# Lower-left blocks of the chunks' inverses two at a time in one product, and the sample rows' queries unpadded, in a GLA and RWKV-7 layer

## The chip, the cores and the metric

The kernel runs on one core of a Trainium2 chip. The metric is the device time of one execution in microseconds. The time before is the median of three runs, 1636.37 us (1636.02 to 1641.12).

## What is computed

One layer of a hybrid decoder for 1024 prompt rows and 8 sample rows of width 1024, all in float32. One input projection feeds two branches, gated linear attention (GLA, 4 heads with keys of 128 and values of 256) and RWKV-7 (16 heads of 64); their outputs go through an up projection each, are merged by gates, projected once more and normalised. The two parts that the change touches, from the reference:

```python
def step(S, inp):                        # RWKV-7, token by token
    rt, wt, kt, vt, kkt, at = inp
    sa = jnp.einsum('bhvk,bhk->bhv', S, -kkt)
    S = S * wt[:, :, None, :] + sa[..., None] * (kkt * at)[:, :, None, :] + vt[..., None] * kt[:, :, None, :]
    y = jnp.einsum('bhvk,bhk->bhv', S, rt)
    return S, y
...
# GLA: S_t = diag(a_t) S_{t-1} + k_t^T v_t ; o_t = q_t S_t
```

For a sample row there is one GLA step: its state (128 x 256 for each row and head) is decayed, gets one outer product added, and is read with the row's query.

## The kernel before, in words

The prompt is worked in two halves of 512 rows; the first half carries the 8 sample rows too (tiles of 260 columns, 512 in the second half). A float32 projection is made of three products in a rounded format, high times high, high times low and low times high (`xh`, `xl`, `whi`, `wlo`): for each piece of 512 weight columns a load `wraw`, a cast to `whi` on ACT and a difference `wlo` on DVE or POOL. In the first half both are also stored, and the second half loads them back.

RWKV-7 runs for 8 pairs of heads in each half, 16 pairs in all. The two heads of a pair lie in partitions 0 to 63 and 64 to 127. For a pair, `front` makes the chunked form: 8 chunks of 64 tokens, in which the recurrence becomes a triangular system. Its matrix's inverse is needed, transposed, in tile `XT` (chunk, head, 64 columns). `front` inverts the diagonal blocks of 32 x 32: it sends them from tile `GG` through memory (`LD`) to a layout with one block per partition, does 31 substitution steps on DVE with the scratch tile `Xt`, and brings the results back through `XD` into `XT`. What is left, the lower-left 32 x 32 block of each 64 x 64 inverse, is made in `back` by two products: the lower-left block of the matrix with one diagonal inverse (`pA`, copied to `As`), then the other diagonal inverse with that (`pZ`, copied to `XT`). Before the change each takes 8 matmuls, one per chunk, with a full 128 x 128 stationary operand and 64 columns streamed: of each head's 64 columns half are of use. `X1` holds the diagonal inverses transposed back, by two transposes of 32 x 256.

After `back`, `turn` transposes what the chain needs and `chain` goes through the 8 chunks one after the other, with three dependent products in tile `pch` each and copies between them.

For the samples, `gla_sample` is part of each of the 4 GLA heads in the first half. It spreads the 8 queries along a diagonal of a zeroed 64-column tile (`qm`), so that each sample's product streams 8 columns of which one isn't zero and all samples add up in one bank `po`. States and values are loaded for two samples at a time.

The order of the work is found by a planner in the program (class `Order`): every part is a stream that yields operations, and at each step the operation with the best key (its estimated start less a priority) is taken and put at the end of its engine's queue. Where an operation can run on two engines, the planner picks one. Buffers and banks come from pools (`big` has three banks). Because estimated starts decide, an edit at one place can move rows on every engine behind it. All DMAs are issued from SP, in order. Every operation is recorded from one line, L215, so the profile is read by tiles: `big<-X,gg` is the first product of `back`, `big<-XT,As` the second, `big<-row` with 8 columns the samples' product, `proj<-xh,whi` and its like the projections, `part,headsr` sums over a head.

Of the kernel before, what the change touches and what calls it, by code (L numbers as in the profile page):

```python
# [402 lines left out]
class Kern(Order):  # L403
# [71 lines left out]
    def setup(self):  # L475
# [65 lines left out]

        for tag, n, bufs in (("az", 4 * HT, 2), ("XT", 2 * HT, 2), ("X1", HT, 1), ("As", 2 * HT, 1)):
# [216 lines left out]
    def gla_head(self, c, h, rows, g):  # L759
# [105 lines left out]
        if c.i:  # L865
            yield S_.dma_start(self.o["gla_p"][0, 0, h], S)
        else:
            yield from self.gla_sample(h, q, k, v, al, [(AT_, z), (km_, vk1)], qp_)
# [24 lines left out]
    def gla_sample(self, h, q, k, v, al, bufs, qm_):  # L893
# [11 lines left out]

        qm = qm_[:, :NS * NS]
        yield E.memset(qm, 0.0)
        yield E.tensor_copy(qm[:, ::NS + 1], q[:, HT:])
# [10 lines left out]
        po = yield from self.bank("big", [P, 2, NS])  # L919
        for n in range(NS // W):  # L920
            Sg, vb = (x[:, :W * GDV].rearrange("p (b v) -> p b v", b=W) for x in bufs[n % 2])
            for w in range(W):
                b = n * W + w
                t = HT + b
                yield A.activation(vb[:, w], vb[:, w], AF.Copy, scale=k[:, t:t + 1])
                yield V.scalar_tensor_tensor(Sg[:, w], Sg[:, w], al[:, t:t + 1], vb[:, w], ALU.mult, ALU.add)
                for j in range(2):
                    yield self.P.matmul(po[:, j], Sg[:, w, j * P:(j + 1) * P], qm[:, NS * b:NS * b + NS],
                                        start=(b == j == 0), stop=(b == NS - 1 and j == 1))
            yield self.S.dma_start(self.o["gla_s"][0, n * W:n * W + W, h].rearrange("b k v -> k b v"), Sg)  # L930
            if n + 2 < NS // W:
                yield from load(n + 2)
        for j in range(2):
            yield self.C.copy(v[j][:, HT:], po[:, j])
        self.free(po)
# [98 lines left out]
    def front(self, c, p, st, d):  # L1034
# [103 lines left out]
        d.AZ, d.BK, d.G, d.XT, d.v, d.bonus, d.pc, d.L = AZ, BK, GG, XT, st[2], st[1], pc, L_  # L1138
        d.y = Pc_[:, :HT]

    def back(self, d):
        GG, XT = d.G, d.XT

        X1_, As_ = (yield from self.get("X1")), (yield from self.get("As"))
        X1 = X1_.rearrange("p (c h t) -> p c h t", c=NCH, h=2)
        As = As_.rearrange("p (c h t) -> p c h t", c=NCH, h=2)
# [12 lines left out]

        for h, hs in enumerate(HS):  # L1160
            yield self.C.copy(XT[q[2 * h], :, h, 32:64], pZ[q[2 * h], :, h])
# [501 lines left out]
```

## Time and profile before

| What | Value |
|---|---|
| median of 3 runs | 1636.37 us |
| profiled execution | 1634.97 us |
| its span, first to last instruction | 1633.0 us |
| mean granted TensorE clock | 0.989 |
| DMA, mean | 193 GB/s |
| DMA issues on SP's queue | 1461 |

One execution was taken by the hardware profiler. "Busy" is the time in which an engine had an instruction running, as a share of the span; a row of a group gives the engine, the operation, the tile written and the tiles read, shapes, the count, then the busy time in microseconds, the mean length of one in ns, and the idle time of the engine just before them with what ended it. The granted clock is the share of TensorE's full clock.

### The profile page before, as it was taken

How to read it: one execution, taken by the hardware profiler on the slowest of the kernel's cores; microseconds unless marked ns; L12 is line 12 of the kernel's file. 1: busy time of each engine (PE TensorE's matmuls, PEld its weight loads, DVE VectorE, ACT ScalarE, POOL GpSimd, SP SyncE). 2: the span in 40 equal slices, each digit the busy share in tenths (PEclk: the TensorE clock that was granted, in tenths of full speed). 3: DMA queues.
4: the chain of work that ended last, by engine and by line, in shares of the span. 5: the costliest groups of instructions: out<-in, count | busy, mean ns of one | idle time of the engine just before them, and what ended most of it. 6: DMA issues, size and time to landing. Idle time of an engine off the chain costs nothing.

```text
span 1633.0 us, 29970 instructions
## 1 busy us (share of the span) xinstructions
PE 1580.9 (97%) x10130; PEld 1404.8 (86%) x10130; DVE 1309.8 (80%) x3396; ACT 880.3 (54%) x2112; POOL 116.0 (7%) x204
## 2 busy tenths in 40 slices
PE   8999999799999998999999999999999999999998
PEld 7899999799999898788888877778878889988786
DVE  7788898889887897679788898989887886656565
ACT  5546766576485757464636472447254758554210
POOL 2100010001000101000000011201000100000000
PEclk9999999899999999999999999999999999999999
DMA  9878775676678556653465446445653577788432
GB/s 292 257 222 251 240 217 157 201 250 191 196 242 264 166 173 210 204 190 120 140 192 161 133 156 200 120 141 178 193 167 117 175 224 253 230 282 270 151 110 84
DMA packets 311924, 315.26 MB, mean 193 GB/s; under 512 B 75363, under 2 KB 197356, under 8 KB 311772
## 3 DMA queue, kind: packets, MB, share of 16 engines
q1 hardware_dynamic: 311772, 313.36, 61.7%
q8 instruction: 80, 1.31, 0.3%
q14 instruction: 72, 0.59, 0.1%
HBM read 195.45 MB, written 117.82 MB: 192 GB/s over the span
## 4 chain that ended last, share of the span: by engine, by line
PE 73%; DVE 14%; DMA 6%; ACT 4%; issue 2%; SPq 1%; POOL 0%; DVEq 0%; POOLq 0%; ACTq 0%
PE proj L215 41%; PE big L215 20%; PE pY L215 7%; PE pch L215 4%; DVE row L215 4%; DVE wide L215 2%; DMA wide<-LD 2%; ACT row L215 1%; DVE X L215 1%; SPq L215 1%; DVE az L215 1%; DMA wraw<-w_in 1%; DVE wlo L215 1%; DVE Xt L215 1%; ACT wide L215 1%
## 5 line engine op out<-in xcount | busy, mean ns | idle before, releaser
L215 PE MATMUL proj<-xh,whi 128*128 128x260 f32 (+1 forms) x1880 | 618.2, 329 | 1.1 <-DVE row L215 0.7
L215 PE MATMUL proj<-xl,whi 128*128 128x260 f32 (+1 forms) x1880 | 617.6, 328 | 0.2 <-DVE xl L215 0.2
L215 PE MATMUL proj<-xh,wlo 128*128 128x260 f32 (+1 forms) x1880 | 616.6, 328 | 0.7 <-POOL wlo L215 0.5
L215 PEld LDWEIGHTS proj<-xh,whi 128*128 128x128 f32 x1880 | 356.6, 190 | 28.5 <-issue 2.6
L215 PEld LDWEIGHTS proj<-xh,wlo 128*128 128x128 f32 x1880 | 356.2, 189 | 26.3 <-issue 2.1
L215 PEld LDWEIGHTS proj<-xl,whi 128*128 128x128 f32 x1880 | 356.4, 190 | 24.8 <-issue 2.6
L215 DVE TENSOR_TENSOR wlo<-wraw,whi 128x512 fp32r<-128x512 f32 x204 | 141.4, 698 | 42.7 <-ACT whi L215 40.3
L215 ACT CAST whi<-wraw 128x512 fp32r<-128x512 f32 x210 | 129.1, 620 | 81.4 <-PE proj L215 34.7
L215 DVE TENSOR_TENSOR row<-row 128x512 f32<-128x512 f32 (+9 forms) x317 | 158.7, 504 | 7.7 <-ACT row L215 3.0
L215 ACT ACTIVATE row<-row 128x512 f32<-128x512 f32 (+5 forms) x229 | 138.3, 611 | 32.5 <-DVE row L215 17.6
L215 DVE TENSOR_TENSOR Xt<-X,wide 128x60 f32<-128x60 f32 (+24 forms) x496 | 104.9, 212 | 31.2 <-DMA wide<-LD 20.5
L215 DVE TENSOR_TENSOR X<-X,Xt 128x60 f32<-128x60 f32 (+24 forms) x496 | 108.2, 218 | 11.4
L215 PE MATMUL big<-row 128*128 128x64 f32 (+4 forms) x712 | 115.0, 278 | 2.1 <-DVE X L215 1.2
L215 ACT ACTIVATE s0p<-wide,pc 64x64 f32<-64x64 f32 x256 | 88.0, 344 | 49.4 <-DVE wide L215 45.4
L215 PEld LDWEIGHTS big<-row 128*128 128x128 f32 (+1 forms) x712 | 97.1, 191 | 7.4 <-DVE row L215 2.7
L215 ACT COPY wide<-pch 64x64 f32<-64x64 f32 x221 | 45.6, 206 | 107.0 <-PE pch L215 103.0
L215 ACT ACTIVATE row<-proj,omu 128x260 f32<-128x260 f32 (+1 forms) x99 | 54.1, 546 | 89.8 <-PE proj L215 84.0
L215 POOL TENSOR_TENSOR row<-row 128x512 f32<-128x512 f32 (+7 forms) x52 | 60.0, 1156 | 560.8 <-DVE row L215 204.5
L215 DVE SCALAR_TENSOR_TENSOR row<-proj,pv,row 128x259 f32<-128x259 f32 (+1 forms) x99 | 56.4, 570 | 34.4 <-ACT tail L215 18.5
L215 ACT COPY wide<-wide 32x256 f32<-32x256 f32 x181 | 73.0, 403 | 18.1 <-DVE wide L215 16.0
L215 DVE SCALAR_TENSOR_TENSOR wide<-pch,pc,s0p 64x64 f32<-64x64 f32 x224 | 63.0, 281 | 21.1 <-PE pch L215 16.8
L215 ACT COPY row<-big 128x128 f32<-128x128 f32 (+7 forms) x162 | 45.4, 309 | 49.1 <-PE big L215 47.4
(259 smaller groups left out, 2770.0 us busy)
## 6 DMA issues: line engine op xcount, KB each, us to landing
wraw<-w_in SPq DMA_DIRECT2D x146, 256.0 KB
wh<-whi SPq DMA_DIRECT2D x146, 256.0 KB
wl<-wlo SPq DMA_DIRECT2D x146, 256.0 KB
whi<-wh SPq DMA_DIRECT2D x146, 256.0 KB
wlo<-wl SPq DMA_DIRECT2D x146, 256.0 KB
wide<-LD SPq DMA_DIRECT2D x64, 128.0 KB
wraw<-w_up_gla SPq DMA_DIRECT2D x32, 256.0 KB
wraw<-w_up_rwkv SPq DMA_DIRECT2D x32, 256.0 KB
```

The lines of the kernel that those rows point to most:

```text
L215: ways.append((eng, lambda call=call: call(out, *args, **kw), price(eng, name, out, args, ins)))
```

## The change

In `front`, six more DMAs per pair. Four bring the lower-left blocks of `GG` into a new tile `L1` (4 x 128 columns, zeroed once): chunk x of the first four and chunk x + 4 of the last four, for both heads, stand in its four 32 x 32 blocks beside the diagonal. Two bring the second diagonal inverse of the last four chunks into the free upper right part of `XT`.

In `back`, both products run over x = 0 to 3 instead of 0 to 7: 4 matmuls of 32 columns with `L1`, and 4 of 64 columns with `As`, which is now 4 x 128 columns. The transposes are 4 of 32 x 128 and go to the scratch tile `Xt`; the tile `X1` is gone. The copies out of each product are 4 of 32 x 128 instead of 2 of 32 x 256.

In `gla_sample`, `qm` with its memset and copy is gone. Each sample's product streams its one query column; a bank of 2 x 2 columns is taken for each group of two samples, copied by two copies of 128 x 2 into the rows' place, and freed, four times a head.

```diff
         for q in range(4):
             yield self.S.dma_start(XD.rearrange("u (i g) t -> g u i t", g=4)[q], X[NU * q:NU * q + NU])
         self.free(X_)
+        L1 = (yield from self.get("L1")).rearrange("p (x t) -> p x t", t=P)
+        H = NCH // 2
+        for h in range(2):
+            for n in range(2):
+                g, to = 2 * h + n, 2 * h + 1 - n
+                yield self.S.dma_start(L1[32 * g:32 * g + 32, :, 32 * to:32 * to + 32],
+                                       GG[64 * h:64 * h + 32, H * n:H * n + H, 0, h, 32:64])
...
+        for h in range(2):
+            yield self.S.dma_start(XT[64 * h:64 * h + 32, 0:H, h, 32:64],
+                                   XD[(2 + h) * NCH + H:(3 + h) * NCH].rearrange("c s t -> s c t"))
...
         for h in range(2):
-            yield self.V.transpose(X1[q[2 * h], :, h], XT[q[2 * h], :, h, 0:32])
-        pA = yield from self.bank("big", [P, NCH, 2, 32])
-        for x in range(NCH):
-            yield self.P.matmul(pA[:, x], GG[:, x, 0], X1[:, x], start=True, stop=True)
+            for n in range(2):
+                yield self.V.transpose(X1[q[2 * h + n]], XT[q[2 * h], H * n:H * n + H, h, 0:32])
+        pA = yield from self.bank("big", [P, H, 32])
+        for x in range(H):
+            yield self.P.matmul(pA[:, x], d.L1[:, x], X1[:, x], start=True, stop=True)
         for h in range(2):
-            yield self.C.copy(As[q[2 * h + 1], :, h, 0:32], pA[q[2 * h + 1], :, h])
-        self.free(pA, X1_)
-        pZ = yield from self.bank("big", [P, NCH, 2, 32])
-        for x in range(NCH):
+            for n in range(2):
+                g = 2 * h + 1 - n
+                yield self.C.copy(As[q[g], :, q[2 * h + n]], pA[q[g]])
+        self.free(pA, X1_, d.L1)
+        pZ = yield from self.bank("big", [P, H, 2, 32])
+        for x in range(H):
             yield self.P.matmul(pZ[:, x], As[:, x], XT[:, x, :, 32:64], start=True, stop=True)
+        for h in range(2):
+            for n in range(2):
+                yield self.C.copy(XT[q[2 * h], H * n:H * n + H, h, 32:64], pZ[q[2 * h + n], :, h])
...
-        qm = qm_[:, :NS * NS]
-        yield E.memset(qm, 0.0)
-        yield E.tensor_copy(qm[:, ::NS + 1], q[:, HT:])
...
         for n in range(NS // W):
+            po = yield from self.bank("big", [P, 2, W])
...
                 for j in range(2):
-                    yield self.P.matmul(po[:, j], Sg[:, w, j * P:(j + 1) * P], qm[:, NS * b:NS * b + NS],
-                                        start=(b == j == 0), stop=(b == NS - 1 and j == 1))
+                    yield self.P.matmul(po[:, j, w:w + 1], Sg[:, w, j * P:(j + 1) * P], q[:, t:t + 1],
+                                        start=(w == j == 0), stop=(w == W - 1 and j == 1))
+            t = HT + n * W
+            for j in range(2):
+                yield self.C.copy(v[j][:, t:t + W], po[:, j])
+            self.free(po)
```

How the planner's order stands now is shown at three places. In its rows `X_184` is the tile `X1`, `L_184` is `L1`, a number ahead of a row is its place on the engine, and xN counts equal instructions in a row.

DVE, third pair of the first half, before: `az_177` and `wide` are the next pair's `front`, `wlo` a piece of weights.

```order
558 L215 SCALAR_TENSOR_TENSOR row<-row,nkk 128x512
559 L215 TENSOR_SCALAR row<-row,pv,oka 128x512
560 L215 TENSOR_TENSOR az_177<-row 64x8x64 x2
561 L215 COPY gg<-az_176 64x8x64 x2
562 L215 SCALAR_TENSOR_TENSOR row<-row 128x512
563 L215 TENSOR_TENSOR row<-row 128x512
564 L215 TENSOR_TENSOR az_177<-row 64x8x64 x2
565 L215 COPY pc<-row 128x8
566 L215 TENSOR_TENSOR wide<-row 64x8x64 x4
567 L215 SCALAR_TENSOR_TENSOR row<-row,pv 128x512
568 L215 TENSOR_TENSOR wlo<-wraw,whi 128x512
```

DVE at the same place now, from a piece of weights ahead of the copy to `As`:

```order
546 L215 TENSOR_TENSOR wlo<-wraw,whi 128x512
547 L215 SCALAR_TENSOR_TENSOR row<-row,pv 128x512 x2
548 L215 CAST l2p<-l2s 128x256
549 L215 COPY As_186<-big 32x4x32
550 L215 SCALAR_TENSOR_TENSOR row<-proj,pv,row 128x251
551 L215 SCALAR_TENSOR_TENSOR row<-bnd,pv,row 128x1
552 L215 SCALAR_TENSOR_TENSOR smp<-shT,pv,row 128x8
553 L215 TENSOR_TENSOR row<-row 128x512
554 L215 TENSOR_TENSOR wlo<-wraw,whi 128x512
555 L215 COPY gg<-az_176 64x8x64 x2
```

Ten rows stood between the copy to `As` (557, not shown) and the next piece of weights; now four stand between, and the next pair's `az` rows come later.

TensorE, second pair of the first half, before: the first product of `back` stands at row 1358, the second here.

```order
1369 L215 MATMUL proj<-xh_199,whi 128x260
1370 L215 MATMUL proj<-xl_217,whi 128x260
1371 L215 MATMUL big<-alr_144,gw_146 128x260
1372 L215 MATMUL big<-XT_181,As_186 128x64 x8
1373 L215 MATMUL big<-alr_144,gw_146 128x260
```

TensorE, the same pair now:

```order
1310 L215 MATMUL proj<-xl_315,whi 128x260
1311 L215 MATMUL proj<-xh_286,wlo 128x260
1312 L215 MATMUL big<-Xt,L_184 128x32 x4
1313 L215 MATMUL big<-XT_181,As_186 128x64 x4
1314 L215 MATMUL proj<-xh_199,whi 128x260
```

Thirteen rows stood between the two products, and none stands there now. The fourth pair has the same neighbours now (rows 2335 and 2336), and the sixth pair had them before.

TensorE at the end of the first half, before, when its projections are used up and the chain's products are left:

```order
3934 L215 MATMUL proj<-xh_286,wlo 128x260
3935 L215 MATMUL pch<-rh,XT_180 128x128
3936 L215 MATMUL pch<-wide 128x128
3937 L215 MATMUL pY<-gg,wide 128x128
3938 L215 MATMUL pch<-wide,gg 128x128
3939 L215 MATMUL pY<-az_176,wide 128x128
3940 L215 MATMUL pch<-rh,XT_180 128x128
3941 L215 MATMUL pch<-wide 128x128
3942 L215 MATMUL pY<-gg,wide 128x128
3943 L215 MATMUL pch<-wide,gg 128x128
```

TensorE there now, where the last projection stands at row 3939 and the products at 3940 to 3944 are those of 3935 to 3939 above:

```order
3945 L215 MATMUL pch<-rh,XT_180 128x128
3946 L215 MATMUL pch<-wide 128x128
3947 L215 MATMUL pY<-gg,wide 128x128
3948 L215 MATMUL pch<-wide,gg 128x128
3949 L215 MATMUL pY<-az_176,wide 128x128
3950 L215 MATMUL pch<-rh,XT_180 128x128
3951 L215 MATMUL big<-part,headsr 128x512
3952 L215 MATMUL pch<-wide 128x128
```

After the last projection five products of `pch` followed the first one (3936, 3938, 3940, 3941, 3943); now it is seven (3941, 3943, 3945, 3946, 3948, 3950, 3952).

More of the change, by code (lines that the diff above doesn't have):

```diff
@@ L540, in setup @@
             nc.gpsimd.memset(t, 0.0)
-        for tag, n, bufs in (("az", 4 * HT, 2), ("XT", 2 * HT, 2), ("X1", HT, 1), ("As", 2 * HT, 1)):
+        for tag, n, bufs in (("az", 4 * HT, 2), ("XT", 2 * HT, 2), ("L1", HT, 1), ("As", HT, 1)):
             ts = [cp.tile([P, n], F32, name=f"{tag}{i}") for i in range(bufs)]
@@ L867, in gla_head @@
         else:
-            yield from self.gla_sample(h, q, k, v, al, [(AT_, z), (km_, vk1)], qp_)
+            yield from self.gla_sample(h, q, k, v, al, [(AT_, z), (km_, vk1)])
         s0, s1 = z, vk1
@@ L891, in gla_head, with gla_sample @@
         self.headed += 1
-    def gla_sample(self, h, q, k, v, al, bufs, qm_):
+    def gla_sample(self, h, q, k, v, al, bufs):
         a, A, V, E = self.a, self.A, self.V, self.E
@@ L918, in gla_sample @@
         yield from load(1)
-        po = yield from self.bank("big", [P, 2, NS])
         for n in range(NS // W):
+            po = yield from self.bank("big", [P, 2, W])
             Sg, vb = (x[:, :W * GDV].rearrange("p (b v) -> p b v", b=W) for x in bufs[n % 2])
@@ L932, in gla_sample @@
                 yield from load(n + 2)
-        for j in range(2):
-            yield self.C.copy(v[j][:, HT:], po[:, j])
-        self.free(po)
     def lora(self, c):
```

10 lines of the change are left out of this document (5 added, 5 removed).

## The prediction

> **What bounds the kernel now.** I read the page first, then the groups by form, then TensorE's timeline around one pair's two products, then the long breaks.
>
> ```profile
> PE 1580.9 (97%) x10130; PEld 1404.8 (86%) x10130; DVE 1309.8 (80%) x3396; ACT 880.3 (54%) x2112; POOL 116.0 (7%) x204
> PEclk9999999899999999999999999999999999999999
> PE 73%; DVE 14%; DMA 6%; ACT 4%; issue 2%; SPq 1%; POOL 0%; DVEq 0%; POOLq 0%; ACTq 0%
> ```
>
> TensorE is busy in 97% of the span and carries 73% of the chain that ended last. Idle are 1633.0 - 1580.9 = 52 us. The large products hardly wait for anything:
>
> ```profile
> L215 PE MATMUL proj<-xh,whi 128*128 128x260 f32 (+1 forms) x1880 | 618.2, 329 | 1.1 <-DVE row L215 0.7
> L215 PE MATMUL proj<-xl,whi 128*128 128x260 f32 (+1 forms) x1880 | 617.6, 328 | 0.2 <-DVE xl L215 0.2
> L215 PE MATMUL proj<-xh,wlo 128*128 128x260 f32 (+1 forms) x1880 | 616.6, 328 | 0.7 <-POOL wlo L215 0.5
> ```
>
> 5640 of them show 2.0 us of idle time in all: operands are there when TensorE comes to them. So the sum is first a count of TensorE's work, then of its few breaks.
>
> **The products of the inverse.** Here are pair 0's two, in TensorE's timeline (start, length, count of records; an f32 matmul leaves two records):
>
> ```profile
> 130.87 0.28 PE L215 MATMUL proj<-xl,whi 128*128 128x260 f32 x1
> 130.99 1.89 PE L215 MATMUL big<-X,gg 128*128 128x64 f32 x16
> 132.69 0.37 PE L215 MATMUL proj<-xh,wlo 128*128 128x260 f32 x1
> ...
> 134.09 0.28 PE L215 MATMUL proj<-xl,whi 128*128 128x260 f32 x1
> 134.21 1.89 PE L215 MATMUL big<-XT,As 128*128 128x64 f32 x16
> 135.91 0.37 PE L215 MATMUL proj<-xh,wlo 128*128 128x260 f32 x1
> ```
>
> From its own start to the next start, each step takes 132.69 - 130.99 = 1.70 us for 8 matmuls, and 1.70 again: 0.106 us a record. The change leaves 4 matmuls of each. The first also shrinks from 64 to 32 columns; what a 32-column record takes, no row shows. It lies between the 64-column row and the 8-column one:
>
> ```profile
> 314.07 0.51 PE L215 MATMUL big<-row 128*128 128x8 f32 x4
> 314.44 0.37 PE L215 MATMUL proj<-xl,whi 128*128 128x260 f32 x1
> ```
>
> That is (314.44 - 314.07)/4 = 0.093 us at 8 columns. Between 8 and 64 columns the pace hardly moves, so I take 0.106: 0.85 us instead of 1.70. With 16 pairs and two steps, 32 x 0.85 = **27.2 us off TensorE**; at 0.093 for the first step it would be 16 x 8 x 0.013 = 1.7 us more.
>
> **The samples' products.** 64 matmuls go from 8 columns to 1. By the two rows above, 56 columns fewer are worth 13 ns, so 7 fewer are worth under 2 ns: 128 records x 2 ns = 0.3 us. I take nothing. What is removed for each of four heads, a memset and a copy on POOL or DVE, frees an engine that is 7% or 80% busy and releases no projection. Added are 24 small copies out of PSUM on ACT or DVE, and the bank is asked for four times in each head instead of being held throughout. ACT has 46% of its time free; nothing taken. If that cover is gone, a copy that is late delays the next group's store and load on SP's queue, and no projection.
>
> **Copies and transposes.** Per pair, 2 transposes become 4 of half the size, and 2 + 2 copies become 4 + 4.
>
> ```profile
> L215 DVE STREAM_TRANSPOSE X<-XT 32x256 f32<-32x256 f32 x32 | 13.8, 432 | 2.1 <-DMA XT<-XD 1.4
> L215 ACT COPY As<-big 32x256 f32<-32x256 f32 x30 | 10.9, 365 | 20.6 <-PE big L215 20.3
> L215 ACT COPY XT<-big 32x256 f32<-32x256 f32 x30 | 10.9, 362 | 25.6 <-PE big L215 25.3
> ```
>
> The transposes now write Xt, the scratch tile of the substitution, so this step of one pair and the substitution of the next could wait for each other.
>
> ```profile
> L215 DVE TENSOR_TENSOR Xt<-X,wide x1: 193/193/193, 164.4 to 164.4; 128x31 f32<-128x31 f32 x1
> ```
>
> Pair 1's substitution starts at 164.4, 28 us after pair 0's second step is over, and in the changed order the 31 steps of a pair and its 4 transposes strictly alternate: nothing. Half-size pieces cost between half and the whole of these: 0 to 0.86 us more of DVE and 0 to 1.45 us more of ACT per pair (4 more copies at no more than 0.363), 23 us of ACT over the kernel at most, inside 750 us in which it is free. On TensorE they count only where the second step stands right behind the first; that is priced below.
>
> **The new DMAs.** 4 + 2 more on SP's queue per pair, 96 in all.
>
> ```profile
> L215 SPq DMA_DIRECT2D XT<-XD x64: 323/450/837, 123.9 to 1351.3; - x64
> ```
>
> ```profile
> SPq L215 <- PE proj L215: 285.0, 128, 8.5
> ```
>
> The first row gives an issue's time (least, median, most), 0.45 us: 2.7 us a pair, 43 us in all. The second says that SP stood 285.0 us behind TensorE's projections, 128 times. All six stand ahead of weight loads and stores. They are covered by the 285 us in which SP itself waits for TensorE to give weight buffers back. I take nothing here; it is the slower rival below.
>
> **The breaks.** The change leaves no row of the schedule where it was, so I price each long break of before and ask the order whether it is still there. Windows: length, busy time of PE, PEld, DVE, ACT, POOL, granted clock.
>
> ```profile
> 288.20:296.90 8.70, 0.25 (x3) 0.04 (x1) 8.59 (x15) 3.31 (x9) 1.28 (x1) 0.63 0.25 92
> 296.90:305.00 8.10, 8.08 (x29) 7.20 (x30) 6.17 (x9) 4.07 (x10) 2.35 (x6) 0.56 0.63 195
> 538.00:550.00 12.00, 10.44 (x62) 10.10 (x61) 11.86 (x20) 7.23 (x18) 1.80 (x2) 0.72 0.41 138
> ...
> 543.00:549.80 6.80, 6.80 (x33) 6.80 (x33) 6.73 (x13) 2.62 (x7) 0.53 (x1) 0.50 0.11 40
> ...
> 640.00:656.00 16.00, 11.23 (x43) 7.46 (x42) 14.41 (x29) 8.75 (x24) 3.90 (x7) 0.68 0.40 129
> ```
>
> At 288 TensorE stands 8.45 us while DVE is full: the stretch of DVE rows 558 to 567, with no piece of weights among them. Then it runs 8.1 us at a clock of 0.56, which loses 8.1 x 0.44 = 3.6 us: 12.0 us. In the changed order the next front starts later and DVE's rows at this place have pieces of weights at 546 and 554; I take the break as gone, **-12.0 us** (ends: 0 and -12.0).
>
> At 538 the second step stands right behind the first:
>
> ```profile
> 538.71 0.28 PE L215 MATMUL proj<-xh,wlo 128*128 128x260 f32 x1
> 539.36 2.00 PE L215 MATMUL big<-X,gg 128*128 128x64 f32 x16 [0.38 <-DVE X L215]
> 542.54 3.30 PE L215 MATMUL big<-XT,As 128*128 128x64 f32 x16 [1.18 <-ACT As L215]
> ```
>
> Idle 12.00 - 10.44 = 1.56 us, clock 12 x 0.28 = 3.4 us: 4.9 us. Before has one such place, after has two (second and fourth pair; rows 1312 and 1313 show the second): **+4.9 us** (ends: 0 and +9.8). Here the clock was 0.50 from 543.0 on, after breaks of 0.38 and 1.18 us. The Trainium skill, "TensorE: Matmul & The Clock Gate", Part 1, speaks against the price: it has the clock halve only after an idle window of about 3.4 us; by that rule such a place would cost its idle 1.6 us, and this term would be +1.6. The measurement decides.
>
> At 640 the first half's projections are used up and the chain runs alone: idle 16.00 - 11.23 = 4.77 us, clock 16 x 0.32 = 5.1 us, over five products of the chain with no projection between them (rows 3936 to 3943): 2.0 us each. After has seven (3941 to 3952): **+4.0 us** (ends: 0 and +6).
>
> Last, a new order brings breaks that I can't point to. I allow one of the size of 538's, **+4.9 us** (ends: 0 and one like 288's, +12.0).
>
> **Sum.** -27.2 - 12.0 + 4.9 + 4.0 + 4.9 = -25.4 us. The profiled execution took 1634.97 us (span 1633.0 and 2.0 around it), so 1609.6; the median of the runs stands 1.4 above it: **1611 us**.
>
> **Rivals.**
> *SP's queue becomes the bound (slower).* 96 issues x 0.45 = 43.2 us. If every one delayed a weight piece for which TensorE then waits, 43.2 - 27.2 = +16: 1652 us. It decides once the lead is used up: in the first half a weight piece serves 24 products 0.12 us apart (130.87 to 130.99 above is one), 2.9 us, so four buffers serve 11.5 us. Six issues are 2.7 us, so the queue must already be 9 us behind. For it: the six come in a burst, some wait for landings. Against: the 2.0 us of idle at the projections, and the 285 us. Chance 0.07.
> *Waits take the gain's place.* DVE is at 80% overall, and at 8.59 of 8.70 us in the break at 288; a faster TensorE meets it more often. Two breaks like 288's that I don't see, 24 us, would leave 1611 + 24 = 1635, no change: 0.07. One, with the 288 break itself still there in another place, 1623: 0.15, still faster.
> *The columns set the pace.* If a record cost what it streams, 0.12/260 = 0.46 ns a column, the first step would save 16 x 0.030 - 8 x 0.015 = 0.36 us a pair and the second 0.24: 9.6 us, with the other terms 1629. The Trainium skill, "TensorE: Matmul & The Clock Gate", section Back-to-back issue gap, lists a floor of about 25 ns for 1 to 64 columns; by it 256 records fewer would be worth an estimated 6.4 us. The rows show 0.106 us at 64 columns and 0.093 at 8, so no pace by column: 0.02.
>
> **How the numbers follow.** The forecast has 0.69. A measurement of this kernel tells about 0.3%, 4.9 us, from no change. Faster by more: 0.69 + 0.15 + 0.02 = 0.86; within: 0.07; slower: 0.07. The lower end takes the break at 288 as gone and nothing new: 1636.4 - 27.2 - 12.0 = 1597, less 2 for a cheaper 32-column record: 1595. The upper end keeps 288's break, the two short places at 9.8 and the boundary at +6, and one small new break of 4.9: 1636.4 - 27.2 + 20.7 = 1630, or 1629 with the cheaper record. About 0.15 is left above, little below.
>
> **What would show it.** Right: 128 records in each of the two groups, the steps 0.85 us from start to next start, some 256 records fewer on TensorE, projections still with about 2 us of idle, no window of 8 us idle in the first 400 us, the first two back-to-back places at a half clock. Wrong: a 32-column step near 0.4 us (columns), SP with far less waiting for TensorE and projections with tens of microseconds of idle behind weight pieces (the queue), or TensorE's idle time grown by 20 us with DVE as releaser (waits).

## The result and the profile after

The changed kernel takes 1652.96 us (median of 5 runs, 1648.70 to 1658.57) against 1637.01 us for the kernel before (5 runs, 1636.02 to 1641.12). The ratio is 1.0104, interval 1.0087 to 1.0120: slower by 16 us, where 25 us faster was forecast.

The page of the changed kernel, its engines' busy times, the granted clock and the chain's shares:

```profile
PE 1570.7 (95%) x9874; PEld 1390.4 (84%) x9874; DVE 1311.1 (79%) x3385; ACT 895.1 (54%) x2210; POOL 143.8 (9%) x223
PEclk9999999999998999899999999999999999999999
PE 66%; DVE 14%; DMA 8%; ACT 5%; SPq 3%; issue 3%; POOL 0%; POOLq 0%; DVEq 0%; ACTq 0%
```

The 256 records are gone as forecast, but TensorE's busy time fell by only 10.2 us. Its idle time rose from 52.1 to 1649.3 - 1570.7 = 78.6 us, and the mean clock fell from 0.989 to 0.980. A lower clock hides in the busy time: 1649.3 x 0.020 = 33.0 us of it, against 1633.0 x 0.011 = 18.0 us before. Busy time less that is TensorE's work at full clock: 1562.9 us before and 1537.7 after. So **25.2 us of work did go**, and 26.5 us of idle time and 15.0 us of clock came, which is the 16.3 us by which the span grew.

TensorE's timeline at pair 0's two products (start, length, count of records):

```profile
134.48 0.98 PE L215 MATMUL big<-Xt,L 128*128 128x32 f32 x8
135.29 0.37 PE L215 MATMUL proj<-xh,whi 128*128 128x260 f32 x1
...
137.18 1.00 PE L215 MATMUL big<-XT,As 128*128 128x64 f32 x8
137.99 0.37 PE L215 MATMUL proj<-xh,whi 128*128 128x260 f32 x1
```

135.29 - 134.48 = 0.81 us and 137.99 - 137.18 = 0.81 us: each step has half its former length, at 32 columns as at 64.

The same view at the second pair, where the two products now stand one behind the other (in brackets: idle before, and what ended it):

```profile
206.56 1.08 PE L215 MATMUL big<-Xt,L 128*128 128x32 f32 x8 [3.12 <-DVE Xt L215]
208.79 1.97 PE L215 MATMUL big<-XT,As 128*128 128x64 f32 x8 [1.15 <-ACT As L215]
```

Windows of the changed kernel (length; busy time of PE, PEld, DVE, ACT, POOL; clock; DMA): the second pair, the place of the old break at 288, the fourth pair, and the end of the first half:

```profile
200.00:214.00 14.00, 9.73 (x61) 9.42 (x60) 12.75 (x21) 7.61 (x20) 3.37 (x3) 0.77 0.63 185
280.00:305.00 25.00, 24.25 (x195) 23.59 (x195) 16.25 (x35) 21.77 (x52) 0.80 (x2) 1.00 0.94 300
372.00:386.00 14.00, 8.57 (x50) 8.23 (x49) 13.81 (x22) 5.35 (x16) 4.46 (x8) 0.76 0.83 253
640.00:672.00 32.00, 26.43 (x144) 20.87 (x144) 24.43 (x54) 18.33 (x48) 3.43 (x7) 0.84 0.42 150
```

The last of these in the kernel before:

```profile
640.00:672.00 32.00, 26.79 (x155) 21.51 (x154) 22.20 (x50) 14.07 (x41) 3.90 (x7) 0.84 0.50 150
```

The break at 288 is gone. The second and fourth pair cost 4.27 + 14 x 0.23 = 7.5 us and 5.43 + 14 x 0.24 = 8.8 us. The end of the first half costs what it did: 5.6 us idle against 5.2, at the same clock.

One more break stands at products of the samples. The same window in the changed kernel and in the kernel before:

```profile
515.00:533.00 18.00, 12.60 (x68) 11.37 (x67) 14.62 (x57) 8.04 (x22) 0.12 (x1) 0.72 0.65 215
```

```profile
515.00:533.00 18.00, 18.00 (x142) 17.37 (x141) 15.76 (x55) 8.69 (x20) 0.00 (x0) 1.00 0.85 266
```

That is 5.4 us of idle time and 18 x 0.28 = 5.0 us of clock, 10.4 us, where before has none. Two of the rows that wait there in the changed kernel, and two of ACT's beside them (`issue` means that the profile shows nothing that was waited for):

```profile
522.61 0.98 PE L215 MATMUL big<-row 128*128 128x1 f32 x4 [2.33 <-issue]
526.25 1.02 PE L215 MATMUL big<-row 128*128 128x1 f32 x4 [1.32 <-DVE row L215]
```

```profile
524.96 0.22 ACT L215 COPY row<-big 128x2 f32<-128x2 f32 x2 [2.58 <-PE big L215]
525.07 0.92 ACT L215 ACTIVATE row<-row 128x256 f32<-128x256 f32 x2
```

ACT's copies out of one group's bank, which the change added, wait for that group's products, and the two rows behind them are part of the next group's states, for which the product at 526.25 waits.

The projections, which waited 2.0 us in all:

```profile
L215 PE MATMUL proj<-xh,whi 128*128 128x260 f32 (+1 forms) x1880 | 620.8, 330 | 9.9 <-DMA whi<-wh 8.0
L215 PE MATMUL proj<-xh,wlo 128*128 128x260 f32 (+1 forms) x1880 | 619.9, 330 | 0.6 <-POOL wlo L215 0.5
L215 PE MATMUL proj<-xl,whi 128*128 128x260 f32 (+1 forms) x1880 | 617.9, 329 | 0.2 <-DVE xl L215 0.2
```

Now they wait 10.7 us, 8.0 of it for weights that the second half loads back. SP's timeline at one of those places, then SP's own wait for TensorE and the issue time of the loads into the tile L1:

```profile
795.05 2.54 SPq L215 DMA_DIRECT2D XD<-X  x4
797.64 2.54 SPq L215 DMA_DIRECT2D L<-gg  x4
800.34 2.91 SPq L215 DMA_DIRECT2D XT<-XD  x6
803.35 0.38 SPq L215 DMA_DIRECT2D whi<-wh  x1
```

```profile
SPq L215 <- PE proj L215: 254.6, 128, 8.3
```

```profile
L215 SPq DMA_DIRECT2D L<-gg x64: 586/600/1809, 119.9 to 1366.1; - x64
```

Fourteen issues stand in one piece, 8.3 us, and the load of `whi` behind them is late, although SP still has 254.6 us in which it waits for TensorE: that free time lies elsewhere.

What one such late load costs, in TensorE's timeline and in windows behind it:

```profile
806.23 0.50 PE L215 MATMUL proj<-xh,whi 128*128 128x512 f32 x1 [2.28 <-DMA whi<-wh]
```

```profile
806.20:808.20 2.00, 1.98 (x13) 1.80 (x14) 0.00 (x0) 0.39 (x2) 0.00 (x0) 1.00 0.73 121
808.20:812.00 3.80, 3.80 (x15) 3.20 (x14) 0.79 (x3) 2.68 (x6) 0.00 (x0) 0.55 1.03 364
812.00:815.00 3.00, 3.00 (x14) 2.42 (x13) 2.97 (x6) 2.71 (x6) 0.00 (x0) 1.00 0.64 203
```

2.28 us of idle time, and 2 us later a mean clock of 0.55 over 3.8 us, another 1.7 us. The kernel has four such waits, 8.0 us, and the clock falls behind each: its mean is 0.81, 0.79, 0.69 and 0.68 over the 9.0, 8.1, 11.0 and 10.6 us that begin with them (from 719.0, 803.9, 1044.0 and 1211.4 us), 10.2 us in all. The Trainium skill, "TensorE: Matmul & The Clock Gate", Part 1, lets the clock halve after an idle window of about 3.4 us; here it fell behind a break of 2.28 us, and the measurement decides. The length of a break alone does not settle it, though. A break of 2.24 us in the same trace left the clock at 1.00:

```profile
918.59 0.46 PE L215 MATMUL pch<-wide 128*128 128x128 f32 x2 [2.24 <-DVE wide L215]
```

```profile
914.00:926.00 12.00, 9.76 (x54) 8.09 (x53) 8.77 (x31) 4.72 (x13) 0.00 (x0) 1.00 0.59 157
```

### The profile page after: what moved, and what is told of

Read it like the earlier page. It is cut to its first block, busy times and chain, and to the rows that moved or that the text cites. A ratio compares the mean times of both kernels' runs of the same rounds, so it can differ in the third digit from the quotient of the medians.

```text
span 1649.3 us, 29754 instructions
## 1 busy us (share of the span) xinstructions
PE 1570.7 (95%) x9874; PEld 1390.4 (84%) x9874; DVE 1311.1 (79%) x3385; ACT 895.1 (54%) x2210; POOL 143.8 (9%) x223
## 4 chain that ended last, share of the span: by engine, by line
PE 66%; DVE 14%; DMA 8%; ACT 5%; SPq 3%; issue 3%; POOL 0%; POOLq 0%; DVEq 0%; ACTq 0%
PE proj L215 36%; PE big L215 19%; PE pY L215 7%; PE pch L215 4%; DVE row L215 4%; SPq L215 3%; DVE wide L215 2%; DVE Xt L215 2%; ACT row L215 2%; ACT wide L215 2%; DMA wide<-LD 2%; DVE X L215 2%; DVE az L215 1%; DMA whi<-wh 1%; DMA l2s<-lora 1%
## 5 line engine op out<-in xcount | busy, mean ns | idle before, releaser
L215 PEld LDWEIGHTS proj<-xl,whi 128*128 128x128 f32 x1880 | 358.3, 191 | 24.4 <-issue 1.7
L215 DVE TENSOR_TENSOR wlo<-wraw,whi 128x512 fp32r<-128x512 f32 x198 | 137.5, 700 | 47.5 <-ACT whi L215 44.5
L215 DVE TENSOR_TENSOR row<-row 128x256 f32<-128x256 f32 (+9 forms) x305 | 153.1, 505 | 8.9 <-ACT row L215 2.2
L215 ACT ACTIVATE row<-row 128x512 f32<-128x512 f32 (+4 forms) x229 | 138.0, 611 | 25.9 <-DVE row L215 15.8
L215 DVE TENSOR_TENSOR Xt<-X,wide 128x60 f32<-128x60 f32 (+24 forms) x496 | 108.5, 219 | 24.3 <-DMA wide<-LD 12.2
L215 POOL TENSOR_TENSOR row<-row 128x512 f32<-128x512 f32 (+6 forms) x64 | 71.0, 1112 | 547.3 <-DVE row L215 279.0
L215 ACT ACTIVATE s0p<-wide,pc 64x64 f32<-64x64 f32 x256 | 88.1, 344 | 42.9 <-DVE wide L215 39.0
L215 ACT COPY wide<-wide 32x256 f32<-32x256 f32 x193 | 77.8, 403 | 18.4 <-DVE wide L215 16.1
L215 DVE SCALAR_TENSOR_TENSOR row<-proj,pv,row 128x259 f32<-128x259 f32 (+1 forms) x99 | 56.4, 570 | 26.3 <-ACT tail L215 13.8
```

The source lines that it names most:

```text
L215: ways.append((eng, lambda call=call: call(out, *args, **kw), price(eng, name, out, args, ins)))
```

## The experiments

Two theories stood at the start: the new order brings the breaks, or the six DMAs per pair do. The run kept_half put a third in their place: TensorE's saved time is not worth its length in this kernel. All runs in numbers follow. The ratios are to the kernel before on the same chip, and the other columns are worked out from the page and the clock of the profiled execution as above (a clock is given to 0.001, so work is good to about 1 us).

| Run | Ratio [95%] | Idle us | Clock loss us | Work at full clock us |
|---|---|---|---|---|
| before | 1 | 52.1 | 18.0 | 1563 |
| after | 1.0104 [1.0087, 1.0120] | 78.6 | 33.0 | 1538 |
| kept_order | 1.0267 [1.0237, 1.0297] | 90.6 | 55.4 | 1532 |
| products_only | 1.0122 [1.0084, 1.0161] | 81.0 | 33.0 | 1536 |
| samples_only | 1.0058 [1.0037, 1.0079] | 56.9 | 18.1 | 1570 |
| no_six | 1.0015 [0.9999, 1.0031] | 69.6 | 27.8 | 1538 |
| planned_without | 1.0049 [1.0029, 1.0069] | 73.7 | 31.1 | 1533 |
| l1_early | 1.0138 [1.0108, 1.0167] | 85.5 | 34.7 | 1533 |
| before_nudge | 1.0074 [1.0046, 1.0102] | 55.7 | 29.6 | 1559 |
| after_nudge | 1.0034 [1.0018, 1.0050] | 72.7 | 31.2 | 1536 |
| kept_half | 0.9993 [0.9979, 1.0006] | 67.8 | 24.4 | 1537 |
| kept_no_six | 1.0023 [1.0009, 1.0038] | 74.4 | 31.2 | 1538 |
| pool_six | 1.0075 [1.0057, 1.0092] | 77.8 | 33.0 | 1537 |
| kept_pool | 1.0100 [1.0078, 1.0123] | 78.6 | 31.3 | 1540 |
| less_dve | 0.9978 [0.9965, 0.9990] | 50.8 | 19.6 | 1561 |
| less_both | 0.9961 [0.9948, 0.9975] | 65.7 | 26.0 | 1534 |
| more_pe | 1.0104 [1.0087, 1.0122] | 42.9 | 16.5 | 1590 |
| after_less | 1.0118 [1.0099, 1.0138] | 74.1 | 41.3 | 1537 |
| no_az | 0.9932 [0.9916, 0.9949] | 46.1 | 17.8 | 1559 |
| no_az_half | 0.9860 [0.9843, 0.9877] | 56.6 | 17.7 | 1535 |

The last column falls into three groups: 1559 to 1570 with whole products, 1532 to 1540 with halved ones, 1590 with half of them doubled. What differs inside a group is idle time and clock.

In several runs the planner is shown an operation of the kernel before, so that the order stays, while other instructions are issued in its place; `put` does that. The pieces of code below are shortened.

**Order or DMAs.** kept_order keeps every engine's order as before and issues the change in it; the new loads go behind old ones.

```diff
-                yield self.S.dma_start(o, x)
+                yield put(self.S.dma_start(o, x), lambda e: (sync.dma_start(o, x), sync.dma_start(lo, li)))
...
-            yield self.P.matmul(pA[:, x], GG[:, x, 0], X1[:, x], start=True, stop=True)
+            yield put(self.P.matmul(pA[:, x], GG[:, x, 0], X1[:, x], ...), lambda e: matmul(pAn[:, x], L1[:, x], Xn[:, x]) if x < H else None)
```

> The planner is shown the operations of before, so every engine keeps the order of before; only what is issued is the change's: 4 matmuls instead of 8 in both steps, the small transposes and copies in place of the large ones, the six DMAs right behind XD's and XT's, the samples' queries one column each (in one bank, copied out at the end as before). Theory 1, the new order makes the breaks: 27 us less work in an order that had few breaks, 1608 to 1618 us. Theory 2, the six DMAs make SP late wherever they stand: no gain, 1635 to 1655 us.

products_only is the changed kernel with the old `gla_sample`, samples_only the kernel before with the new one:

```diff
-            yield from self.gla_sample(h, q, k, v, al, [(AT_, z), (km_, vk1)], qp_)
+            yield from self.gla_sample(h, q, k, v, al, [(AT_, z), (km_, vk1)])
```

> The change's products and DMAs with the samples as before; the planner is free. Theory 1: yet another order, so anywhere between a full gain and the loss of after, 1610 to 1655 us, with the loss in breaks at other places than in after. Theory 2: the DMAs are all there, 1640 to 1655 us, with projections of the second half waiting for whi as in after.

> The samples' edit alone with before's products; the planner is free. Work on TensorE is that of before. Theory 1: before's time moved by breaks of the new order alone, 1630 to 1650 us. Theory 2: no DMA is added, so before's time, 1635 to 1639 us.

no_six keeps the changed kernel's order but doesn't issue the six DMAs:

```diff
-                yield self.S.dma_start(L1[...], GG[...])
+                yield put(self.S.dma_start(L1[...], GG[...]), lambda e: None)
...
-            yield self.S.dma_start(XT[...], XD[...])
+            yield put(self.S.dma_start(XT[...], XD[...]), lambda e: None)
```

> The order of after, but the six DMAs of each pair are not issued, so the lower-left blocks are left out (L1 stays zero). Theory 1: the breaks stay where the order put them, 1640 to 1650 us. Theory 2: SP is as free as before, the gain of 27 us appears, 1610 to 1625 us.

Measured: 1680.01, 1657.32, 1645.38 and 1638.19 us beside 1637.14 us. The order of before does not save the change: kept_order is the slowest of all. Only samples_only came as one theory had it, the first; kept_order and products_only stand above both ranges, and no_six between its two. The six DMAs cost 1.0104 - 1.0015 = 0.9%, 15 us, in the changed order. Taking them away brings back the time of before and not the 25 us below it. The samples' part, taken at nothing, costs 0.6% alone. Its work column stands 7 us higher, which nothing here explains, and a new break stands in TensorE's timeline:

```profile
554.90 0.80 PE L215 MATMUL big<-part,headsr 128*128 128x512 f32 x1 [8.04 <-DVE part L215]
```

**Order alone.** planned_without takes the six DMAs out for the planner too; l1_early moves the four loads of L1 right behind those of `L`, ahead of the substitution; the nudges change one number of the planner.

```diff
             yield self.S.dma_start(L_[NU * q:NU * q + NU], LD.rearrange("n c s t -> (n c) (s t)"))
+        L1 = (yield from self.get("L1")).rearrange("p (x t) -> p x t", t=P)
...
+                yield self.S.dma_start(L1[32 * g:32 * g + 32, :, 32 * to:32 * to + 32],
+                                       GG[64 * h:64 * h + 32, H * n:H * n + H, 0, h, 32:64])
```

```diff
-HOLD = 0.11
+HOLD = 0.12
```

> The change without the six DMAs of a pair, and the planner doesn't see them either, so it makes its order without them (the lower-left blocks are left out). Theory 1, the luck of a new order: any order may have after's breaks, 1625 to 1650 us. Theory 2, SP: in after the six DMAs also push the planned times of weights and of XT back, and so put TensorE's rows where they break; without them the whole gain shows, 1605 to 1618 us.

> The change with the four loads of L1 issued right behind LD's loads, before the substitution, instead of in the burst between XD and XT; XT's two stay. Theory 1: one more order, 1625 to 1655 us. Theory 2: the burst ahead of XT and of the weights is 10 issues instead of 14, XT lands about 2.5 us earlier, most of the gain appears, 1612 to 1630 us.

> Before with one price of the planner changed by 0.01 us (HOLD, 0.11 to 0.12), so the same instructions in another order: the spread that the order alone makes. Theory 1: 10 us or more away from before, either way. Theory 2: within 5 us of it.

> After with the same price changed, so the change's instructions in another order. Theory 1: 10 us or more away from after, either way. Theory 2: within 5 us of after, 1648 to 1658 us, with projections of the second half waiting for whi at the same bursts.

Measured: 1641.27, 1655.13, 1645.17 and 1638.37 us beside 1633.54 us. The same nudge makes the kernel before 0.7% slower and the changed one 1.0104 - 1.0034 = 0.7% faster: an order is worth some 12 us either way, with no change of the work. Theory 1 fits all four, l1_early at the very end of its range. In l1_early no projection waits for a loaded weight, and other breaks stand in the place of those waits (17.9 us ended by DVE's `part`, 13.4 by ACT's `wide`). None of the four is faster than before.

**The credit by itself.** kept_half is the cleanest: order of before, nothing added, the matmuls of chunks 4 to 7 not issued.

```diff
+            op = self.P.matmul(pA[:, x], GG[:, x, 0], X1[:, x], start=True, stop=True)
+            yield op if x < H else put(op, lambda e: None)
```

> The kernel before in its own order, with one thing taken away: of both products of the inverse only the matmuls of chunks 0 to 3 are issued, and the copies out of them take only those chunks; the lower-left blocks of chunks 4 to 7 are left out. No new DMA, the same transposes, the same samples' products. This is the credit of the forecast by itself, 32 x 0.85 = 27.2 us of TensorE. If TensorE's work sets the end, as the forecast has it: 1637 - 27 = 1610 us, at most 4.9 us more for a break or two. If the other engines set the pace (rival, the waits take the gain's place): within 10 us of 1637, with TensorE's idle time grown by 20 us or more.

1635.61 us beside 1635.48: no gain at all. The rival was right, though idle time grew by 15.7 us and not by the 20 it named; clock, 6.4 us, took more of the rest. TensorE's timeline of kept_half around pair 0 shows how:

```profile
133.29 1.10 PE L215 MATMUL big<-XT,As 128*128 128x64 f32 x8
134.21 0.37 PE L215 MATMUL proj<-xh,wlo 128*128 128x260 f32 x1
...
141.29 0.39 PE L215 MATMUL proj<-xh,whi 128*128 128x260 f32 x1 [0.97 <-ACT row L215]
...
149.69 0.49 PE L215 MATMUL big<-part,headsr 128*128 128x512 f32 x1 [0.70 <-DVE part L215]
```

The same two rows in the kernel before:

```profile
141.86 0.28 PE L215 MATMUL proj<-xh,whi 128*128 128x260 f32 x1
...
149.88 0.50 PE L215 MATMUL big<-part,headsr 128*128 128x512 f32 x1 [0.44 <-DVE part L215]
```

Behind the second step kept_half is 135.91 - 134.21 = 1.70 us early. At 141.29 it waits 0.97 us for ACT, whose row there stands behind copies that had waited 3.06 us for DVE, and is 0.57 us early; at 149.69 it waits for DVE's sum and is 0.19 us early, no more than it was ahead of the first product. Matched so instruction by instruction, over windows of 20 us, kept_half is nowhere more than 6 us ahead of before. DVE has no room there, as one window shows (busy time of PE, PEld, DVE, ACT, POOL) in before and then in kept_half:

```profile
131.00:141.30 10.30, 10.30 (x91) 10.30 (x90) 10.15 (x16) 6.13 (x13) 2.34 (x6) 1.00 0.61 190
```

```profile
131.00:141.30 10.30, 9.32 (x78) 8.90 (x76) 10.15 (x16) 5.75 (x14) 2.34 (x6) 1.00 0.60 192
```

DVE's 10.15 us of 10.30 are the same; TensorE only stands still more.

**The DMAs' price by queue.** kept_no_six is kept_order without the six DMAs; pool_six and kept_pool issue them from GpSimd.

```diff
-                yield self.S.dma_start(L1[...], GG[...])
+                yield put(self.S.dma_start(L1[...], GG[...]), lambda e: self.nc.gpsimd.dma_start(L1[...], GG[...]))
```

> The run kept_order without its six DMAs per pair: the order of before, the change's 4 + 4 matmuls, 4 transposes, 4 + 4 copies and the samples' single columns; the lower-left blocks' loads are left out, so those blocks are not computed. If the six DMAs were what made kept_order 43 us slower than before: 1610 us, as far below before as the products' 27.2 us. If the smaller transposes and copies are late for TensorE in this order: 1637 us or more, with the idle time at the first product as in kept_order (28.5 us).

> The changed kernel in its own order, with the six DMAs per pair issued from GpSimd's queue instead of SP's. If it is the time that they take and wait on SP's queue ahead of weight loads: as the changed kernel without them, 1638 us, and no idle time at projections behind whi. If it is the transfers themselves (landing, or what the products wait for): as the changed kernel, 1653 us.

> The run kept_order with its six DMAs per pair on GpSimd's queue: the order of before, the change whole. If SP's queue was what cost 43 us there: 1610 to 1620 us, faster than before and the changed kernel. If the first product waits for the landing of its operands, whoever issues them: 1660 us or more, with the idle time at the first product still over 20 us.

Measured: 1639.88, 1648.76 and 1652.11 us beside 1635.48. In the order of before the six cost 1.0267 - 1.0023 = 2.4%, 40 us, from SP, and 1.0100 - 1.0023 = 0.8%, 13 us, from GpSimd. The group of the first product in kept_order, kept_no_six and kept_pool (behind the second bar: idle time before it):

```profile
L1189 PE MATMUL big<-X,L 128*128 128x32 f32 x128 | 21.5, 316 | 28.6 <-issue 16.0 <-DVE X L1182 12.5
```

```profile
L1189 PE MATMUL big<-X,L 128*128 128x32 f32 x128 | 16.8, 273 | 4.1 <-DVE X L1182 3.8
```

```profile
L1190 PE MATMUL big<-X,L 128*128 128x32 f32 x128 | 17.0, 274 | 4.6 <-issue 2.7 <-DVE X L1183 1.6
```

28.6 - 4.1 = 24.5 us of idle time at this product, and 55.4 - 31.2 = 24.2 us of clock over the kernel, come with the six DMAs on SP's queue (TensorE's idle time as a whole grows by 16.2 us), where they stand between the transfers that the first product waits for. From GpSimd that wait is all but gone. In the changed order the products stand later (134.48 us at pair 0, 130.99 before), and the queue costs less: pool_six is 1.0104 - 1.0075 = 0.3%, 5 us, below the changed kernel, and its projections wait for no weights:

```profile
L215 PE MATMUL proj<-xh,whi 128*128 128x260 f32 (+1 forms) x1880 | 621.8, 331 | 1.8 <-ACT row L215 1.8
```

The other 1.0075 - 1.0015 = 0.6%, 10 us, stay with the six DMAs on another queue. But GpSimd's queue has a price of its own at the end of the program. Here are GpSimd's DRAINs, among its last instructions, in pool_six and in no_six (least, median, most in ns):

```profile
L1687 POOLq DRAIN  x3: 34/102/8757, 1638.3 to 1647.6; - x3
```

```profile
L1687 POOLq DRAIN  x3: 39/78/886, 1631.9 to 1635.3; - x3
```

The longest takes 8.76 us instead of 0.89 (8.75 in kept_pool, 0.89 in kept_no_six). From the end of GpSimd's work to the end of the span it is 8.7 us in pool_six and 2.8 in no_six, so 5.9 of these 10 us, and of the 13 in the order of before, come behind all the work. TensorE's last product, in no_six, the changed kernel and pool_six, leaves them out:

```profile
1627.64 0.28 PE L215 MATMUL pY<-whi,xl 128*128 128x256 f32 x1
```

```profile
1641.40 0.27 PE L215 MATMUL pY<-whi,xl 128*128 128x256 f32 x1
```

```profile
1634.04 0.28 PE L215 MATMUL pY<-whi,xl 128*128 128x256 f32 x1
```

The changed kernel is 13.8 us behind no_six there, and pool_six 6.4 us, of which 2.2 us stand in the first 20 us, ahead of the first of these DMAs. (In the order of before this product starts at 1635.73 us in kept_pool and in kept_no_six alike, though this trace of kept_no_six is of its slowest run.) no_six has the changed kernel's order, so their TensorE instructions can be matched one by one: the changed kernel falls behind by 3.4 us from 719 to 727 us, by 3.6 from 804 to 812 and by 4.2 from 1211 to 1222, at three of the four places where a projection waits for `whi`. At the fourth no_six has a break of its own, 4.27 us ahead of a first product.

So of the 15 us in the changed order about half or more is SP's queue: 13.8 - 6.4 = 7.4 us by these traces, 5 + 5.9 = 11 us by the medians. For the other 4 to 8 us no cause is shown, and runs of one kernel lie as far apart (kept_no_six from 1634.33 to 1645.51 us). None of the expectations held as it stood, and both no_six and kept_no_six, with no DMA added, have no gain.

**What sets the pace.** less_dve leaves out substitution steps 12 to 19, less_both does that in kept_half, after_less in the changed kernel; more_pe issues the matmuls of chunks 4 to 7 twice.

```diff
-            yield V.tensor_add(X[:, 0:ni, j + 1:], X[:, 0:ni, j + 1:], tv)
+            op = V.tensor_add(X[:, 0:ni, j + 1:], X[:, 0:ni, j + 1:], tv)
+            yield put(op, lambda e: None) if 12 <= j < 20 else op
```

> The kernel before in its own order, with 8 of the 31 substitution steps of each pair not issued on DVE (steps 12 to 19, a multiplication and an addition each, so the inverses are incomplete): 16 x 8 x 2 x 0.213 = 54.5 us less work on DVE, TensorE's work the same. If DVE sets the pace between the pairs: faster than before by 15 us or more, 1610 to 1622 us, with TensorE's idle time under 45 us. If TensorE and its clock set it: within 5 us of 1637.

> less_dve and kept_half together: 8 substitution steps and the matmuls of chunks 4 to 7 of both products left out, the order of before. If DVE sets the pace and now has room: less_dve less most of 27.2 us, 1585 to 1600 us, so that the products' work counts here and not in kept_half. If whatever TensorE wins is lost again to its own breaks and clock: the time of less_dve, within 5 us.

> The kernel before in its own order with the matmuls of chunks 4 to 7 of both products issued twice: 27.2 us more of TensorE work, nothing else changed, the same result. If TensorE's work sets the pace as the forecast had it: 1637 + 27 = 1664 us. If the other engines set it in those stretches: a good part is free, 1640 to 1652 us. If the two are level (a balanced queue), less work brings nothing and more work costs all of it: 1664 us too, so this run tells how much room there is above, not below.

> The changed kernel in its own order with the same 8 substitution steps left out, 54.5 us less work on DVE. If it was DVE's pace that ate the gain: clearly below less_dve, by 10 us or more of the 27.2 (the six DMAs stay). If the change's losses have their own cause (the six DMAs, the order): as far above less_dve as the changed kernel stands above before, 16 us.

Measured: 1633.11, 1628.97, 1652.37 and 1654.39 us beside 1636.40. The 54.5 us less of DVE's work (its busy time, in which neighbours overlap, falls by 1309.8 - 1264.3 = 45.5 us) give 0.2%, so DVE's total is not the bound either, and with it the halved products give 0.9978 - 0.9961 = 0.2%, 3 us. 27 us more of TensorE's work cost 1.0%, 17 us: the rest fills idle time (42.9 us left). after_less gains nothing over the changed kernel. less_dve and less_both missed the numbers of "DVE sets the pace" and met the other branch, within 5 us of 1637 and of less_dve. after_less stands 1.0118 - 0.9978 = 1.4%, 23 us, above less_dve, further than the 16 us of its second branch; more_pe stands at the upper end of "a good part is free". Whether the place of DVE's work counts was left open.

no_az and no_az_half take 62 rows of 773 ns, 48 us, out of DVE's rows between the products and the sums over a head (DVE's busy time falls by 1309.8 - 1270.4 = 39.4 us).

```diff
-            yield E.tensor_mul(AZ[hs, :, 0, h], bc(ta)[hs], Pc[hs, :, 0:C])
+            yield put(E.tensor_mul(AZ[hs, :, 0, h], bc(ta)[hs], Pc[hs, :, 0:C]), lambda e: None)
```

> The kernel before in its own order, without the 64 products that make the az tile in front (62 on DVE, 47.9 us, two on POOL; the tile stays zero, so the decayed keys and queries of RWKV-7 are left out). On DVE they lie in the stretch ahead of the sums and copies that TensorE and ACT wait for. If DVE's rows in that stretch set the pace: faster than less_dve, 1615 to 1628 us. If the place of DVE's work does not matter: like less_dve, 1633 us.

> no_az and kept_half together: no az products, and the matmuls of chunks 4 to 7 of both products left out. If DVE's stretch behind the products took the gain in kept_half: below no_az by most of 27.2 us, 1590 to 1608 us, and TensorE's breaks at the sums over a head (18.9 us of idle in kept_half) under 12 us. If other waits take it again: within 8 us of no_az.

1625.43 and 1613.36 us beside 1637.14. The place counts: 0.7% where less_dve with more work removed had 0.2%. And now the halved products are worth 0.9932 - 0.9860 = 0.7%, 12 us, where alone they were worth nothing. TensorE's first sum over a head behind pair 0's products in no_az, then in no_az_half:

```profile
147.80 0.40 PE L215 MATMUL big<-part,headsr 128*128 128x512 f32 x1
```

```profile
146.26 0.40 PE L215 MATMUL big<-part,headsr 128*128 128x512 f32 x1
```

No wait stands there, and 1.54 us of the 1.70 are still to be seen. The group of these sums over the whole kernel, in kept_half and no_az_half:

```profile
L215 PE MATMUL big<-part,headsr 128*128 128x512 f32 x128 | 57.1, 453 | 18.9 <-ACT part L215 10.0 <-DVE part L215 7.6 <-ACT row L215 1.0
```

```profile
L215 PE MATMUL big<-part,headsr 128*128 128x512 f32 x128 | 54.9, 437 | 8.8 <-ACT part L215 6.7 <-DVE part L215 1.9
```

So for this part it is shown: DVE's rows behind the products took part of the gain. 12 us came back of the 1559 - 1535 = 24 us of work that went, between the two expectations. Of the other 12, 10.5 us are idle time again (46.1 to 56.6), some 6 us of it ended by DVE and 4 by ACT. Which of their rows would have to come earlier for the whole gain stays open. No complete version here beats the kernel before.

## Why the prediction was wrong

**The products** were right as work: 0.81 us a step for the forecast 0.85, and 25.2 us of full-clock work gone for 27.2. **As time the term failed**: "So the sum is first a count of TensorE's work, then of its few breaks." kept_half is this term alone, forecast -27.2 us, measured 0.9993, nothing. The projections' 2.0 us of idle time did show that operands were there, but by how little they were there no row of idle time shows. A TensorE that comes 1.7 us earlier meets DVE or ACT within 15 us and waits. The rival "Waits take the gain's place" had this mechanism, at 0.07 and 0.15, as a few big breaks; it came as many small ones. Its sign came too: TensorE's waits that DVE ended add up to 43 us in the changed kernel and 23 before.

**The new DMAs**, "I take nothing here", failed too. They cost 15 us in this order. Their issue takes 0.60 us, not 0.45 (L1's loads), and "covered by the 285 us" set a total against a burst: 14 issues in a row are 8.3 us, and SP's free time lies elsewhere. The slower rival, at 0.07, had this mechanism: late weights behind a burst, 10.7 - 2.0 = 8.7 us more of idle time at the projections, and 10.2 us of clock (more than 15 in sum, as no_six has a break of its own at one of these places). That its 1652 us is so near the measured 1652.96 is luck. It set 43.2 us for issues that all delay TensorE against a full gain of 27.2 us, and neither came.

**The breaks.** 288's is gone as forecast (-12.0). The back-to-back places came where the order showed them, but at 7.5 and 8.8 us instead of 4.9 each: +11.4 beside the one of before, for +4.9. The end of the half was forecast +4.0 and measured +0.4: seven products in a row instead of five were no longer. The unknown breaks were the largest error among these: from 16.3 = -25.2 - 12.0 + 11.4 + 0.4 + 8.7 + rest, the rest is 33.0 us, where 4.9 was allowed and 12.0 was the end. 10.4 us of it are the place at 515 to 533 us, and 10.2 us the clock behind the late weights. The 12.4 us left need not come from the order: kept_half, in the old order, has 15.7 us more idle time and 6.4 us more clock loss than before, the gain given back.

**The samples** were taken at nothing, since a late copy would delay "no projection". At 515 to 533 us it did: the late products of the samples stand ahead of projections in TensorE's queue. How much of the 10.4 us there the copies make, and how much the order, is not shown. samples_only is 0.6% slower, no more than what before_nudge makes by order alone; products_only, without these copies, is at 1.0122, so the two do not add up, and the samples' own part in the 16 us is not told apart from order.

**Copies and transposes**: kept_no_six less kept_half is 0.3%, 5 us, for 4 + 4 smaller copies, 4 transposes and the samples' columns in the order of before, where nothing was taken.

The Trainium skill, "Perfetto Trace Analysis", section Identifying Performance Opportunities, advises improving the engine with the highest occupancy first, and for TensorE it prefers the busy share of the weight loads to that of the products. By either, 86% or 97% against DVE's 80%, TensorE was the right one; kept_half, 27 us less of its work for nothing, speaks against that here. The same section's second advice, to look at what the gaps of that engine wait for and make that faster, agrees with no_az, 0.7% faster.

## What to carry to other kernels

An engine that is busy 97% of the time and hardly waits can still be only level with the others: before crediting removed work, follow one saved stretch forward in the trace to the next place where the engine's operands come from elsewhere, and ask by how much those were early. A cheap test is a kernel in the same order that leaves out just that work. DMAs added to an in-order queue are priced as a burst against the next load behind them, not against the queue's total free time. A test run that moves them to another queue brings that queue's own costs, so the place where the work ends is compared too, and not only the time.

## What was not expected of the hardware

Behind a break of 2.28 us the mean clock fell to 0.55 over 3.8 us, about 2 us after TensorE had started again (806 to 812 us); a break of 2.24 us at 916 us left it at 1.00. So short breaks can cost more than their length: the changed kernel has 26.5 us more idle time, and 15.0 us more clock loss with it.

Matmuls of 32 columns take as long as those of 64, 0.101 us a record (0.81 / 8).

Six DMAs per pair on GpSimd's queue make its DRAIN at the end of the program take 8.76 us instead of 0.89, and end the execution 5.9 us later.

An order of instructions alone, moved by one planner constant, is worth 12 us (0.7%), more than twice the 0.3% that a measurement tells apart. Of its two orders the kernel before has the better one.
